# Seven block products in place of eight for part of gate and up, in both FFNs of a hybrid decoder layer

## Chip, cores and metric

One core of a Trainium2 chip. The metric is the time of one execution on the device in microseconds; smaller is better. Engines: TensorE (PE; PEld is its weight load), VectorE (DVE), ScalarE (ACT), GpSimd (POOL), and SyncE (SP), which issues DMAs.

## The reference, cut

256 tokens of width 2048 pass a SwiGLU half-step FFN, a stage of token mixers (convolution, latent attention, attention to memory, gates), and a second FFN. All is f32. The two FFNs are what the change touches:

```
def swiglu_ffn(h, w_gu, w_down):
    g, u = jnp.split(h @ w_gu, 2, axis=-1)
    return (jax.nn.silu(g) * u) @ w_down
x = x + 0.5 * swiglu_ffn(rmsnorm(x, g_ffn1[l]), w_ffn1_gu[l], w_ffn1_down[l])
...
x = x + 0.5 * swiglu_ffn(rmsnorm(x, g_ffn2[l]), w_ffn2_gu[l], w_ffn2_down[l])
```

`w_gu` is 2048 x 11264 (gate and up, 5632 columns each), `w_down` 5632 x 2048.

## The kernel before

Every f32 product is made of three passes in a reduced f32 type: both operands are split into a rounded part (h) and the rest (l), and h·h, l·h and h·l are summed in PSUM. Activations are the stationary operand (128 channels x 128 tokens), weights the moving one (128 x 512).

`linear` works off 512 output columns for the two token tiles: per chunk of two k tiles, `chunk` loads 512 KB of weights (`raw`, 4 buffers), ScalarE casts them to `wh` (line 139), VectorE subtracts for `wl` (line 141), and TensorE runs lines 163 to 165 per k tile and token tile. Two sums stand in two of four PSUM banks (`acc`), so the next `linear` starts in the other two.

`gate_up` takes 11 blocks of 512 columns. For each it calls `linear` for gate (16 k tiles), has ScalarE apply silu with the norm's factor (394), calls `linear` for up, and has VectorE multiply (398). `block_T` then turns the product h on TensorE (213) and splits it (192, 193), by deferred pieces: `defer` puts a closure into a queue that `tick` works off as chunks go by. In the first FFN's first block, `load_x` also loads x and has it turned; `setup_mixer` (constants and tables of the mixers) runs ahead of the silu of block 1. Then four `linear` calls with 44 k tiles take w_down, and add to x, which stays in SBUF.

The order of instructions on each engine is fixed ahead of time by a scheduler that takes what is ready, in program order; what is `pinned` keeps program order on its engine. Each engine works off its own queue in order. Tiles named `gen` share 32 buffers of 4 KB per partition; `misc` are four PSUM banks.

The mixers run between 545 and 1650 us; in them VectorE does the convolution with 360 operations (line 652) beside the splits of weights.

## Time and profile before

| what | value |
|---|---|
| median of 3 runs | 2455.03 us (2454.24 to 2455.8) |
| span of the profiled execution | 2454.7 us |
| TensorE, VectorE, ScalarE busy | 2443.1, 1415.3, 1129.7 us |
| matmuls, all forms | 11126 |
| mean DMA rate | 189 GB/s |

A busy share is an average over stages. Durations of matmuls overlap in the records, so their cost is read from start to start. A wait says which engine's instruction ended last before another could start.

### The profile page before, as it was taken

Reading aid. Unit: us, or ns where it says so; the run is one execution under the profiler, and the core shown is the slowest. Engines: PE = TensorE matmul, PEld = TensorE weight load, DVE = VectorE, ACT = ScalarE, POOL = GpSimd, SP = SyncE. Lnnn points to the kernel's source line nnn. Section 1 sums busy time; section 2 is a strip of 40 time slices with the busy share of each in tenths; the row PEclk is TensorE's granted clock in tenths of the full one; section 3 lists DMA queues with packets and bytes.
Section 4 is the critical chain, followed back from the end, with each engine's and each line's share of the span. In section 5 each row is a group of like instructions: output and inputs, shape, how many; then the busy total and the mean of one; then the engine's idle time right before and its main releaser. Section 6 shows DMA issues by size and latency. Waiting matters only on the chain.

```text
span 2454.7 us, 29412 instructions
## 1 busy us (share of the span) xinstructions
PE 2443.1 (100%) x11126; PEld 2025.3 (83%) x11126; DVE 1415.3 (58%) x1772; ACT 1129.7 (46%) x1476; POOL 77.5 (3%) x173
## 2 busy tenths in 40 slices
PE   8999999999999999999999999999999999999999
PEld 7888888888888889888888888888888888888887
DVE  5545545444445999975555576565545545444443
ACT  6444444444444455444556564344444444443332
POOL 2000000000000000000212100000000000000000
PEclk9999999999999999999999999999999999999999
DMA  7566666666667656565555567656666566666664
GB/s 244 184 192 191 188 190 189 189 189 199 200 200 231 188 182 181 187 195 150 173 151 168 163 180 239 198 182 186 189 189 189 188 190 192 186 191 192 200 203 138
DMA packets 240879, 463.63 MB, mean 189 GB/s; under 512 B 14752, under 2 KB 22544, under 8 KB 240736
## 3 DMA queue, kind: packets, MB, share of 16 engines
q1 hardware_dynamic: 236288, 449.89, 58.8%
q0 software_dynamic: 3264, 9.75, 1.4%
q10 hardware_dynamic: 1184, 2.11, 0.2%
q8 instruction: 87, 1.43, 0.2%
q14 instruction: 56, 0.46, 0.1%
HBM read 457.49 MB, written 4.19 MB: 188 GB/s over the span
## 4 chain that ended last, share of the span: by engine, by line
PE 97%; issue 2%; DMA 1%; POOL 0%; ACT 0%; SPq 0%; DVE 0%; POOLq 0%
PE acc L163 31%; PE acc L165 31%; PE acc L164 31%; PE misc L213 1%; PE misc L883 1%; DMA x<-in_x_dram 0%; PE misc L882 0%; PE misc L791 0%; PE misc L759 0%; POOL junk L274 0%; PE misc L863 0%; PE misc L912 0%; PE misc L905 0%; DMA junk<-in_g_mknorm_dram 0%; PE misc L745 0%
## 5 line engine op out<-in xcount | busy, mean ns | idle before, releaser
L141 DVE TENSOR_TENSOR wl<-raw,wh 128x1024 fp32r<-128x1024 f32 (+2 forms) x859 | 1043.9, 1217 | 935.8 <-ACT wh L139 930.4
L139 ACT CAST wh<-raw 128x1024 fp32r<-128x1024 f32 (+2 forms) x859 | 899.1, 1048 | 1183.8 <-PE acc L164 1124.4
L163 PE MATMUL acc<-wh,tH 128*128 128x512 f32 (+3 forms) x3200 | 1251.5, 391 | 1.4 <-ACT wh L139 1.4
L165 PE MATMUL acc<-wl,tH 128*128 128x512 f32 (+3 forms) x3200 | 1239.3, 387 | 0.0
L164 PE MATMUL acc<-wh,tL 128*128 128x512 f32 (+3 forms) x3200 | 1238.3, 387 | 0.0
L165 PEld LDWEIGHTS acc<-wl,tH 128*128 128x128 f32 x3200 | 601.8, 188 | 122.3
L163 PEld LDWEIGHTS acc<-wh,tH 128*128 128x128 f32 x3200 | 601.9, 188 | 121.7 <-issue 2.7
L164 PEld LDWEIGHTS acc<-wh,tL 128*128 128x128 f32 x3200 | 602.3, 188 | 117.6
L652 DVE SCALAR_TENSOR_TENSOR y<-aT,cw,y 128x256 f32<-128x256 f32 x360 | 150.2, 475 | 0.0
L394 ACT ACTIVATE sg<-acc,r 128x512 f32<-128x512 f32 x44 | 30.1, 690 | 25.2 <-PE acc L165 21.8
L195 ACT ACTIVATE tH<-misc,gains 128x256 fp32r<-128x256 f32 x56 | 26.0, 473 | 27.0 <-DVE tL L196 27.0
L163 PE MATMUL acc<-wh,oH 128*128 128x512 f32 x96 | 38.0, 395 | 0.0
L165 PE MATMUL acc<-wl,oH 128*128 128x512 f32 x96 | 37.4, 390 | 0.0
L164 PE MATMUL acc<-wh,oL 128*128 128x512 f32 x96 | 37.4, 389 | 0.0
L163 PE MATMUL acc<-wh,yH 128*128 128x512 f32 x96 | 37.3, 389 | 0.0
L164 PE MATMUL acc<-wh,yL 128*128 128x512 f32 x96 | 37.3, 389 | 0.0
L165 PE MATMUL acc<-wl,yH 128*128 128x512 f32 x96 | 37.3, 389 | 0.0
L193 DVE TENSOR_TENSOR tL<-misc,tH 128x512 fp32r<-128x512 f32 x44 | 30.1, 684 | 3.3 <-PE misc L213 3.3
L398 DVE SCALAR_TENSOR_TENSOR h<-acc,r,sg 128x512 f32<-128x512 f32 x44 | 31.4, 750 | 0.1
L196 DVE SCALAR_TENSOR_TENSOR tL<-misc,gains,tH 128x256 fp32r<-128x256 f32 x56 | 26.4, 479 | 8.7 <-ACT tH L195 8.7
L213 PEld LDWEIGHTS misc<-ident,h 128*128 128x128 f32 x176 | 21.8, 139 | 5.7
L213 PE MATMUL misc<-ident,h 128*128 128x128 f32 x176 | 26.3, 272 | 0.0
(215 smaller groups left out, 889.9 us busy)
## 6 DMA issues: line engine op xcount, KB each, us to landing
raw<-in_w_ffn_gu_dram SPq DMA_DIRECT2D x351, 512.0 KB, 3.5
raw<-in_w_ffn_down_dram SPq DMA_DIRECT2D x176, 512.0 KB, 4.1
raw<-in_w_in_dram SPq DMA_DIRECT2D x172, 512.0 KB, 3.7
raw<-in_w_mem_kv_dram SPq DMA_DIRECT2D x32, 512.0 KB, 4.2
raw<-in_w_out_dram SPq DMA_DIRECT2D x32, 512.0 KB, 3.7
raw<-in_w_conv_out_dram SPq DMA_DIRECT2D x24, 512.0 KB, 4.9
raw<-in_w_mla_out_dram SPq DMA_DIRECT2D x24, 512.0 KB, 4.1
raw<-in_w_mem_out_dram SPq DMA_DIRECT2D x16, 512.0 KB, 3.7
```

Source lines behind the costliest of these rows:

```text
L139: self.pinned(nc.scalar.copy(wh, raw))
L141: self.pinned(nc.vector.tensor_tensor(out=wl, in0=raw, in1=wh.bitcast(F32), op=ALU.subtract))
L163: nc.tensor.matmul(ps[tt], xh[:, t], wh[:, j, :], start=st, stop=False)
L164: nc.tensor.matmul(ps[tt], xl[:, t], wh[:, j, :], start=False, stop=False)
L165: nc.tensor.matmul(ps[tt], xh[:, t], wl[:, j, :], start=False, stop=sp)
L193: nc.vector.tensor_tensor(out=l, in0=src, in1=h.bitcast(F32), op=ALU.subtract)
L195: nc.scalar.activation(out=h, in_=src, func=AF.Identity, scale=scale)
L196: nc.vector.scalar_tensor_tensor(out=l, in0=src, scalar=scale, in1=h.bitcast(F32), op0=ALU.mult, op1=ALU.subtract)
L213: nc.tensor.transpose(ps[:, j, tt * P:(tt + 1) * P], src[:, tt, (j0 + j) * P:(j0 + j + 1) * P], self.ident)
L394: nc.scalar.activation(out=sg[:, tt], in_=pg[tt], func=AF.Silu, scale=rstd[:, tt:tt + 1])
L398: nc.vector.scalar_tensor_tensor(out=h[:, tt], in0=pu[tt], scalar=rstd[:, tt:tt + 1], in1=sg[:, tt], op0=ALU.mult, op1=ALU.mult)
L652: nc.vector.scalar_tensor_tensor(out=y, in0=aT[ch // 3][:, ch % 3, k:k + S], scalar=self.cw[:, ch, k:k + 1], in1=y, op0=ALU.mult, op1=ALU.add)
```

## The change

Gate and up of a block are now computed together, as one product over pairs of k tiles: 2 token tiles x 2 k tiles times 2 k tiles x (gate, up). `group` handles 8 pairs per block and keeps four sums F in all four `acc` banks. A plain pair takes 8 block products as before. In blocks 1 to 10 the pairs 0, 1 and 2 are computed with seven block products: `pair_chunk` forms four sums of weights on VectorE (three additions) and splits seven blocks of 512 columns; `pair_forms` forms the sums of the activations once per FFN, during block 0, after `prepare` has scaled x by the norm's factor; four of the seven products are summed in the four `misc` banks (`first`), three go to F (`second`); `remainders` makes the corrections E out of the four banks, and the end of the block adds E to F. The order of a block is Strassen, Strassen, plain, Strassen, four plain; `second` of the first pair comes behind `first` of the second.

Around it: weights are loaded 1 MB per pair into three `raw` slots; six slots each of `h` and `l`; one `t`. `ffn_stage` and `mix_stage` lay the same SBUF bytes out anew for the FFNs and for w_down with the mixers, where the slots have the old sizes. `gen` has 25 buffers, and seven more (`gen2`) lie in the mixers' layout. h is turned unsplit (`turn`, in the next block), and split by `h_fn` during the first `linear` of w_down; the first two weight chunks of w_down are made ahead of block 10's end. x is scaled in place, so it is loaded anew in the first FFN, and written to and read from DRAM (`xd2`) in the second. `setup_mixer`'s loads move to `load_mixer` after block 0; the rest runs after block 1 as before.

```diff
-NB_RAW = 4
-NB_H = 5
-NB_L = 5
-NB_GEN = 32
+NB_GEN = 25
+PAIRS = D // (2 * P)
+STRASSEN = (0, 1, 2)
+FFN_PLACES = [("raw", 8192)] * 3 + [("h", 4096)] * 6 + [("l", 4096)] * 6 + [("t", 6144), ("h4", 2048), ("h4", 2048),
+                                                                            ("l4", 2048), ("l4", 2048)]
...
+    def pair_chunk(self, W3, pr, b, seven, first=False):
...
+        def split(src, tags, n):
+            h = self.slot(tags[0], [n, CB], F32R)
+            self.pinned(nc.scalar.copy(h, src))
+            l = self.slot(tags[1], [n, CB], F32R)
+            self.pinned(nc.vector.tensor_tensor(out=l, in0=src, in1=h.bitcast(F32), op=ALU.subtract))
+            return [(h[:, i], l[:, i]) for i in range(n)]
...
+            return split(raw[:, 0:2], "hl", 2) + split(raw[:, 2:4], "hl", 2)
+        nc.sync.dma_start(out=raw[:, 0:2], in_=W3[ka, :, cs])
+        nc.sync.dma_start(out=raw[:, 2], in_=W3[kb, 1, cs])
+        nc.sync.dma_start(out=raw[:, 3], in_=W3[kb, 0, cs])
+        t = self.slot("t", [3, CB], F32)
+        add = lambda o, x, y: self.pinned(nc.vector.tensor_tensor(out=o, in0=x, in1=y, op=ALU.add))
+        add(t[:, 0:2], raw[:, 0:2], raw[:, 1:3])
+        add(raw[:, 1], t[:, 0], raw[:, 2])
+        add(t[:, 2], raw[:, 1], raw[:, 3])
+        b11, t2 = split(raw[:, 0:2], "hl", 2)
+        t1, t3 = split(t[:, 0:2], "hl", 2)
+        b22, b21 = split(raw[:, 2:4], "hl", 2)
+        (t4,) = split(t[:, 2:3], ("h4", "l4"), 1)
+        return b11, t2, t1, t3, b21, t4, b22
+    def pair_forms(self, xn, pr, g):
...
+        seven = pr in STRASSEN
+        ps = self.misc().rearrange("p (j t) -> p j t", j=4)
+        o = 2 * (pr % 2)
+        for j, (k, tt) in enumerate(((0, 0), (0, 1), (1, 1), (1, 0)) if seven else ((0, 0), (0, 1), (1, 0), (1, 1))):
...
+        x = self.gen([7, P], F32, "xf")
+        for k in range(2):
+            nc.scalar.activation(out=x[:, 2 * k:2 * k + 2], in_=ps[:, 2 * k:2 * k + 2], func=AF.Identity,
+                                 scale=g[:, 2 * pr + k:2 * pr + k + 1])
+        if not seven:
...
+            return [[(hl[:, 0, 2 * k + tt], hl[:, 1, 2 * k + tt]) for tt in range(2)] for k in range(2)]
+        v = nc.vector
+        v.tensor_tensor(out=x[:, 4:6], in0=x[:, 1:3], in1=x[:, 0:2], op=ALU.subtract)
+        v.tensor_tensor(out=x[:, 6], in0=x[:, 5], in1=x[:, 0], op=ALU.add)
+        v.tensor_tensor(out=x[:, 1], in0=x[:, 3], in1=x[:, 6], op=ALU.subtract)
+        h = self.gen([7, P], F32R, "xsH")
+        l = self.gen([7, P], F32R, "xsL")
...
+    def group(self, W3, b, forms, order, mid=None):
...
+        def first(w, f):
+            b11, t2, t1, t3, b21, t4, b22 = w
+            if not Q:
+                Q.extend(self.misc() for _ in range(4))
+                self.n7 = 0
+            st, sp = self.n7 == 0, self.n7 == n7 - 1
+            self.n7 += 1
+            for q, x, y in zip(Q, ("a11", "s6", "s5", "s7"), (b11, t2, t1, t3)):
+                self.mul(q, f[x], y, st, sp)
+        def second(w, f):
+            b11, t2, t1, t3, b21, t4, b22 = w
+            for i, x, y in ((0, "a12", b21), (1, "a22", t4), (2, "s3", b22)):
+                left[i] -= 1
+                put(i, f[x], y, left[i] == 0)
+        E = None
+        waiting = []
+        done = 0
+        for pos, (pr, seven) in enumerate(order):
+            f = forms(pr)
+            w = self.pair_chunk(W3, pr, b, seven, b == 0 and pos == 0)
+            if seven:
+                first(w, f)
+                done += 1
+                if pos == 0 and n7 > 1:
+                    waiting.append((w, f))
+                else:
+                    for a in waiting:
+                        second(*a)
+                    waiting = []
+                    second(w, f)
+            else:
+                plain(pr, w, f)
+            if n7 and done == n7 and E is None and not waiting:
+                E = self.remainders(Q)
+                Q = None
+            self.tick(4.0)
+            if mid is not None:
+                mid(pos)
+        return F, E
+    def remainders(self, Q):
...
+        E = self.slotE()
+        nc.scalar.copy(E[:, 0], p1)
+        v.tensor_tensor(out=E[:, 1], in0=q6, in1=E[:, 0], op=ALU.subtract)
+        v.tensor_tensor(out=E[:, 2], in0=E[:, 1], in1=p5, op=ALU.subtract)
+        v.scalar_tensor_tensor(out=E[:, 1], in0=E[:, 1], scalar=-1.0, in1=p7, op0=ALU.mult, op1=ALU.subtract)
+        v.tensor_tensor(out=E[:, 3], in0=E[:, 2], in1=p7, op=ALU.add)
+        def prepare(c):
+            rstd = self.get(rstd_)
+            xn = xs[c]
+            for tt in range(2):
+                nc.scalar.activation(out=xn[:, tt], in_=xn[:, tt], func=AF.Identity, scale=rstd[:, tt:tt + 1])
+            for pr in (2 * c, 2 * c + 1):
+                forms[pr] = self.pair_forms(xn, pr, gain)
+        def mid0(pos):
+            if mid is not None:
+                mid(pos)
+            if PAIRS - 5 <= pos < PAIRS - 1:
+                prepare(pos - (PAIRS - 5))
...
+        order0 = [(pr, False) for pr in range(PAIRS)]
+        rest = [pr for pr in range(PAIRS) if pr not in STRASSEN]
+        mixed = [(STRASSEN[0], True), (STRASSEN[1], True), (rest[0], False), (STRASSEN[2], True)]
+        mixed += [(pr, False) for pr in rest[1:]]
         for b in range(D_FF // CB):
-            pg = self.linear(W, b * CB, CB, xT, D // P, before if b == 0 else None)
-            rstd = self.get(rstd_)
-            if b == 1 and between is not None:
-                between()
+            if b == 0:
+                F, E = self.group(W3, b, plain_forms, order0, mid0)
+                rstd = self.get(rstd_)
+                scale = lambda tt: rstd[:, tt:tt + 1]
+            else:
+                F, E = self.group(W3, b, forms.get, mixed)
+            if between is not None and b < 2:
+                between[b]()
+            if b + 1 == D_FF // CB:
+                self.flush()
+                self.mix_stage()
+                hidden = self.h_fn(hT)
+                hidden(0)
+                ahead = [self.chunk(W_down, k0, 2, 0, CB) for k0 in (0, 2)]
             sg = self.gen([2, CB], F32, "sg")
-            for tt in range(2):
-                nc.scalar.activation(out=sg[:, tt], in_=pg[tt], func=AF.Silu, scale=rstd[:, tt:tt + 1])
-            pu = self.linear(W, D_FF + b * CB, CB, xT, D // P)
             h = self.gen([2, CB], F32, "h")
             for tt in range(2):
-                nc.vector.scalar_tensor_tensor(out=h[:, tt], in0=pu[tt], scalar=rstd[:, tt:tt + 1], in1=sg[:, tt],
-                                               op0=ALU.mult, op1=ALU.mult)
-            hT.append(self.block_T(h, lambda j: None, 1.5, 1.0))
-        return hT
+                if E is None:
+                    nc.scalar.activation(out=sg[:, tt], in_=F[tt], func=AF.Silu, scale=scale(tt))
+                else:
+                    nc.vector.tensor_tensor(out=sg[:, tt], in0=F[tt], in1=E[:, tt], op=ALU.add)
+                    nc.scalar.activation(out=sg[:, tt], in_=sg[:, tt], func=AF.Silu)
+            for tt in range(2):
+                if E is None:
+                    nc.vector.scalar_tensor_tensor(out=h[:, tt], in0=F[2 + tt], scalar=scale(tt), in1=sg[:, tt],
+                                                   op0=ALU.mult, op1=ALU.mult)
+                else:
+                    nc.vector.tensor_tensor(out=h[:, tt], in0=F[2 + tt], in1=E[:, 2 + tt], op=ALU.add)
+            if E is not None:
+                nc.vector.tensor_tensor(out=h, in0=h, in1=sg, op=ALU.mult)
+            self.defer(4.0 * 5 - 1 if b + 1 < D_FF // CB else 1.0, lambda h=h: turn(h))
+        return hidden, ahead
+        self.ffn_stage()
         for c in range(NCB):
-            ps = self.linear(d["w_ffn2_down"], c * CB, CB, self.xT_fn(hT), D_FF // P)
-            for tt in range(2):
-                nc.vector.scalar_tensor_tensor(out=xs[c][:, tt], in0=ps[tt], scalar=0.5, in1=xs[c][:, tt],
+            nc.gpsimd.dma_start(out=xd2[c], in_=xs[c])
+        hidden, ahead = self.gate_up(d["w_ffn2_gu"], blocks, xs, self.g_ffn2, rstd, d["w_ffn2_down"])
+        for c in range(NCB):
+            x = self.gen([2, CB], F32, "x2")
+            nc.gpsimd.dma_start(out=x, in_=xd2[c])
```

## Rows read from the trace of the kernel before

**Rows 1.** Page, parts 1 and 4: engines' busy time; shares of the chain.
```profile
PE 2443.1 (100%) x11126; PEld 2025.3 (83%) x11126; DVE 1415.3 (58%) x1772; ACT 1129.7 (46%) x1476; POOL 77.5 (3%) x173
...
PE acc L163 31%; PE acc L165 31%; PE acc L164 31%; PE misc L213 1%; PE misc L883 1%; DMA x<-in_x_dram 0%; PE misc L882 0%; PE misc L791 0%; PE misc L759 0%; POOL junk L274 0%; PE misc L863 0%; PE misc L912 0%; PE misc L905 0%; DMA junk<-in_g_mknorm_dram 0%; PE misc L745 0%
```

**Rows 2.** Page, part 5: line, xcount | busy us, mean ns | idle.
```profile
L163 PE MATMUL acc<-wh,tH 128*128 128x512 f32 (+3 forms) x3200 | 1251.5, 391 | 1.4 <-ACT wh L139 1.4
```

**Rows 3.** Waits, 45 to 485 us: total us, times, longest.
```profile
ACT wh L139 <- PE acc L164: 234.1, 144, 2.2
DVE wl L141 <- ACT wh L139: 207.0, 142, 1.6
```

**Rows 4.** Timeline of PE: start us, us, engine, line; 17 rows, first and last.
```profile
430.28 0.39 PE L165 MATMUL acc<-wl,tH 128*128 128x512 f32 x1
...
433.91 0.39 PE L163 MATMUL acc<-wh,tH 128*128 128x512 f32 x1
```

**Rows 5.** Timeline of PE around a group of transposes.
```profile
115.11 0.39 PE L165 MATMUL acc<-wl,tH 128*128 128x512 f32 x1
115.34 0.60 PE L213 MATMUL misc<-ident,h 128*128 128x128 f32 x4
...
116.01 0.39 PE L164 MATMUL acc<-wh,tL 128*128 128x512 f32 x1
```

**Rows 6.** VectorE's groups, shapes apart (columns as in rows 2).
```profile
L141 DVE TENSOR_TENSOR wl<-raw,wh 128x1024 fp32r<-128x1024 f32 x839 | 1024.8, 1224 | 923.3 <-ACT wh L139 917.8 <-PE misc L745 1.5
L460 DVE TENSOR_TENSOR x<-acc,x 128x512 f32<-128x512 f32 x8 | 5.5, 690 | 0.0
L658 DVE TENSOR_TENSOR lns<-y,y 128x1024 f32<-128x1024 f32 x1 | 1.2, 1215 | 0.0
```

**Rows 7.** Stretches: us, busy us (count) by engine, clock, DMA share.
```profile
820.00:1020.00 200.00, 200.00 (x994) 170.22 (x993) 199.97 (x377) 109.50 (x180) 3.77 (x6) 1.00 0.61 184
45.00:485.00 440.00, 439.73 (x1985) 363.44 (x1984) 227.16 (x239) 187.13 (x199) 1.01 (x2) 1.00 0.61 191
```

**Rows 8.** Timeline of VectorE in the convolution.
```profile
899.71 1.22 DVE L141 TENSOR_TENSOR wl<-raw,wh 128x1024 fp32r<-128x1024 f32 x1
900.85 1.67 DVE L652 SCALAR_TENSOR_TENSOR y<-aT,cw,y 128x256 f32<-128x256 f32 x4
```

**Rows 9.** ScalarE's groups, shapes apart (columns as in rows 2).
```profile
L139 ACT CAST wh<-raw 128x1024 fp32r<-128x1024 f32 x839 | 882.4, 1053 | 1162.1 <-PE acc L164 1105.5 <-issue 33.3 <-ACT e L893 4.7
L192 ACT CAST tH<-misc 128x512 fp32r<-128x512 f32 x44 | 25.6, 581 | 0.0
L195 ACT ACTIVATE tH<-misc,g 128x256 fp32r<-128x256 f32 x16 | 7.4, 472 | 8.4 <-PE misc L213 7.9 <-DVE tL L196 0.6
L139 ACT CAST wh<-raw 128x512 fp32r<-128x512 f32 x2 | 1.2, 617 | 0.5 <-DMA raw<-in_w_ffn_gu_dram 0.5
```

**Rows 10.** Timeline of ScalarE: one sum of squares.
```profile
28.02 0.63 ACT L185 ACTIVATE junk<-x 128x512 f32<-128x512 f32 x1
```

**Rows 11.** Timeline of the start, all engines, rows picked.
```profile
7.09 0.79 PE L163 MATMUL acc<-wh,tH 128*128 128x512 f32 x1 [1.44 <-ACT wh L139]
...
7.93 0.62 ACT L139 CAST wh<-raw 128x512 fp32r<-128x512 f32 x1 [0.52 <-DMA raw<-in_w_ffn_gu_dram]
...
14.82 0.66 PE L213 MATMUL misc<-ident,x 128*128 128x128 f32 x4 [2.24 <-DMA x<-in_x_dram]
...
20.01 0.48 PE L163 MATMUL acc<-wh,tH 128*128 128x512 f32 x1
```

**Rows 12.** Stretch of the start (columns as in rows 7).
```profile
16.00:19.40 3.40, 3.40 (x10) 2.61 (x9) 2.64 (x4) 2.45 (x3) 0.00 (x0) 0.51 1.05 386
```

**Rows 13.** Timeline of VectorE in the set-up of the mixers.
```profile
85.03 0.15 DVE L290 TENSOR_TENSOR g_nope<-gains 128x1 f32<-128x1 f32 x1
...
99.49 0.18 DVE L380 TENSOR_SCALAR ropeS<-ropeS 128x64 f32<-128x64 f32 x1
```

**Rows 14.** Page, part 6: issues, count, KB each, us to landing.
```profile
raw<-in_w_ffn_gu_dram SPq DMA_DIRECT2D x351, 512.0 KB, 3.5
```

More of the change, by code (lines that the diff above doesn't have):

```diff
@@ L86, in __init__, with ffn_stage @@
         self.pin = True
+    def ffn_stage(self):
+        old = self.rings
+        names = [t for t, _ in FFN_PLACES]
+        self.places(FFN_PLACES)
+        order = {t: [i for i, n in enumerate(names) if n == t] for t in dict.fromkeys(names)}
+        if old is not None:
+            for t, w, o in (("h", "wh", 3), ("l", "wl", 9)):
+                held = [p - o for p in self.was[w]]
+                order[t] = [o + i for i in [i for i in range(6) if i not in held] + held]
+        self.rings = order
+        self.place_of_g = None
@@ new lines, in places, with at @@
+    def places(self, sizes):
+        if self.slots is not None:
+            if self.place_of_g is not None:
+                for w in ("wh", "wl"):
+                    self.was[w] = [self.where[i] for i in self.rings[w]]
+            self.slots.close()
+        self.slots = ExitStack()
+        self.pools = [self.slots.enter_context(self.tc.tile_pool(name=self.nm(t), bufs=1)) for t, _ in sizes]
+    def at(self, i, shape, dt, name):
+        return self.pools[i].tile([P] + list(shape), dt, tag="p", name=self.nm(name))
@@ L148, in linear @@
         step = max(2, 1024 // N)
-        k0s = list(range(0, nk, step))
-        if before is not None:
-            k0s.insert(1, 1)
-        for k0, k1 in zip(k0s, k0s[1:] + [nk]):
-            if before is not None:
-                before(k0)
-            kk = k1 - k0
-            wh, wl = self.chunk(W, k0, kk, c0, N)
+        ahead = list(ahead)
+        for k0 in range(0, nk, step):
+            kk = min(step, nk - k0)
+            wh, wl = ahead.pop(0) if ahead else self.chunk(W, k0, kk, c0, N)
             for j in range(kk):
@@ new lines, in group, with put, plain @@
+    def group(self, W3, b, forms, order, mid=None):
+        nc = self.nc
+        F = [self.acc() for _ in range(4)]
+        begun = set()
+        n7 = sum(s for _, s in order)
+        left = {0: len(order), 1: len(order), 2: len(order), 3: len(order) - n7}
+        Q = []
+        def put(i, x, w, last):
+            self.mul(F[i], x, w, i not in begun, last)
+            begun.add(i)
+        def plain(pr, w, f):
+            for i in range(4):
+                left[i] -= 1
+            for k in range(2):
+                for g in range(2):
+                    for tt in range(2):
+                        i = 2 * g + tt
+                        put(i, f[k][tt], w[2 * k + g], k == 1 and left[i] == 0)
+        def first(w, f):
[10 more added lines that the diff above has]
+            for i, x, y in ((0, "a12", b21), (1, "a22", t4), (2, "s3", b22)):
+                left[i] -= 1
+                put(i, f[x], y, left[i] == 0)
[24 more added lines that the diff above has]
+        return F, E
@@ L438, in run, with load_x, turn_x, mid @@
-        hT = self.gate_up(d["w_ffn1_gu"], self.xT_fn(blocks), rstd, load_x, self.setup_mixer)
+        def load_x(c):
+            x = self.gen([2, CB], F32, "x")
+            n = CB // 2 if c == 0 else CB
+            for o in range(0, CB, n):
+                self.pinned(nc.sync.dma_start(out=x[:, :, o:o + n], in_=x_v[:, :, c * CB + o:c * CB + o + n]), True)
+            xs.append(x)
+        def turn_x(c):
+            blocks.append(self.block_T(xs[c], self.gains("g_ffn1", c), 0.0, 0.1))
+        def mid(pos):
+            self.pin = False
+            self.pin_dma = pos < 4
+            if pos < 3:
+                load_x(pos + 1)
+            if pos in (0, 2, 4):
+                turn_x(pos // 2 + 1)
+            if pos == 2:
+                self.stats(xs, D, 0.1, 0.1, True, rstd)
@@ L439, in run @@
+        (self.g_ffn1,) = self.load_gains([d["g_ffn1"]], "g1", nc.scalar)
+        load_x(0)
+        turn_x(0)
+        hidden, ahead = self.gate_up(d["w_ffn1_gu"], blocks, xs, self.g_ffn1, rstd, d["w_ffn1_down"], mid,
+                                     (self.load_mixer, self.setup_mixer))
         xd = [self.dp.tile([P, 2, CB], F32, tag=f"xd{c}", name=f"xd{c}") for c in range(NCB)]
+        xd2 = [self.dp.tile([P, 2, CB], F32, tag=f"xe{c}", name=f"xe{c}") for c in range(NCB)]
         blocks = []
+        xs = []
@@ L441, in run @@
         for c in range(NCB):
-            ps = self.linear(d["w_ffn1_down"], c * CB, CB, self.xT_fn(hT), D_FF // P)
+            x = self.gen([2, CB], F32, "x")
+            nc.gpsimd.dma_start(out=x, in_=x_v[:, :, c * CB:(c + 1) * CB])
+            xs.append(x)
+            ps = self.linear(d["w_ffn1_down"], c * CB, CB, hidden, D_FF // P, ahead if c == 0 else ())
             for tt in range(2):
```

189 lines of the change are left out of this document (147 added, 42 removed).

## The prediction

> **What bounds the kernel now.** I read the page first: TensorE is busy for the whole span, and the chain that ended last lies for 93% of the span on lines 163 to 165, the three passes of `linear` [rows 1]. VectorE (58%) and ScalarE (46%) have room on average [rows 1]. The groups of instructions then say how many matmuls these are: 3200 on each of the three lines, 9600 [rows 2]. The waits of ten FFN blocks confirm the direction: ScalarE waits for TensorE to free a `wh`, VectorE waits for ScalarE, and no wait of TensorE is among the long ones [rows 3]. So a matmul less is time less, as long as nothing else becomes late.
>
> The price of a matmul is not its mean of 391 ns, because records overlap. In the timeline 16 starts lie between 430.28 and 433.91 us [rows 4]: 3.63 / 16 = 0.227 us each. A group of four transposes, between two matmuls that start at 115.11 and 116.01 with one other in between, costs 0.90 - 2 x 0.227 = 0.45 us [rows 5]; its first follower starts late, and that is in it.
>
> **TensorE: removed and added.** One FFN block (512 gate and 512 up columns) now has 16 k tiles x 2 token tiles x 2 x 3 passes = 192 matmuls. After the change a plain pair has 24 and a Strassen pair 7 x 3 = 21, so blocks 1 to 10 have 5 x 24 + 3 x 21 = 183. Block 0 keeps 192. Removed: 9 x 10 blocks x 2 FFNs = 180 matmuls, 180 x 0.227 = **40.9 us**. Added: `pair_forms` transposes x a second time, 8 groups of four in each FFN, 16 x 0.45 = **7.2 us**. The transposes of h stay two groups per block. TensorE's time per mixed block is then 183 x 0.227 + 2 x 0.45 = 42.4 us, against 44.5 us. Net: -33.7 us, if TensorE stays fed.
>
> **VectorE: the new load.** Prices: a 1024-wide weight split 1.224 us, a 1024-wide f32 add 1.215, a 512-wide one that reads PSUM 0.690 [rows 6]; all 512-wide work is taken at 0.69. A plain pair is two splits, 2.45 us. A Strassen pair has the three weight additions, 1.215 + 2 x 0.69 = 2.60, and splits of 1024, 1024, 1024 and 512, 3 x 1.224 + 0.69 = 4.36: together 6.96 us. Per mixed block: 5 x 2.45 + 3 x 6.96 = 33.1; `remainders` 4 x 0.69 = 2.8; the end of the block 4 x 0.69 + 1.22 = 4.0. Sum 39.9 us in 40 instructions. In ten blocks of before VectorE is busy for 227 of 440 us, 52% [rows 7]; it goes to 39.9 / 42.4 = 94% of a block.
>
> Is that a bound? The stage where the convolution runs is the nearest row: from 820 to 1020 us VectorE is busy for 199.97 of 200 us, and TensorE for all 200 [rows 7]. A full VectorE therefore need not stop TensorE, if its order serves TensorE's weights first. And a full VectorE is faster than the sum of its durations: there a split starts at 899.71 and the next instruction at 900.85, 1.14 us later, though it lasts 1.22 [rows 8]. With 0.08 us of overlap at each of 40 instructions the block costs 36.7 us, 87% of TensorE's. I take no stall in the steady blocks. From below there is no gain to be had, since TensorE's waits there are already nil [rows 3]; the upper end is the rival below.
>
> The Trainium skill has a rule against this change. "VectorE: DVE Perf Modes", § The DRAIN you can't avoid, says that each operation is followed by a flush of roughly its duration less 266 ns before the next starts, and that chaining does not avoid it. By that rule, as an estimate, a mixed block would hold VectorE for about 39.9 + (39.9 - 40 x 0.266) = 69 us, and it would be the bound. This trace disagrees: the 1.14 us from start to start [rows 8] leave no room for a flush outside the recorded duration.
>
> **ScalarE.** Casts: plain pair 2 x 1.053, Strassen pair 3 x 1.053 + 0.617; `E`'s copy 0.58, two copies of h 2 x 0.58 [rows 9], two silu out of SBUF 2 x 0.63, as a square of the same size [rows 10]. Per mixed block 10.5 + 11.3 + 0.6 + 1.2 + 1.3 = 24.9 us of 42.4: hidden. The exception is block 0 of the first FFN. There `prepare` scales x (8 x 0.63), takes it turned out of PSUM (16 x 0.47), casts seven or four forms per pair (896 wide between 0.617 and 1.053, so 3 x 0.94, and 5 x 0.62), and this meets the sums of squares (8 x 0.63), the splits of x (16 x 0.47) and the block's own 16 casts (16.8). Sum 5.0 + 7.5 + 5.9 + 5.0 + 7.5 + 16.8 = 47.7 us against TensorE's 192 x 0.227 + 8 x 0.45 + 2.7 = 49.9 us. It has up to 6 `h` slots, three pairs, of lead. From 0 to 4 us; I take 1. In the second FFN x is turned earlier and the sum is 47.7 - 7.5 = 40 us: 0.
>
> **What is moved.** (a) The start. Now the first matmul starts at 7.09 us, on a 256 KB weight; the second weight's cast starts at 7.93 [rows 11]. After, the first cast takes gate and up of a k tile, 512 KB, and lasts 1.05: 7.93 + 1.05 = 9.0, 1.9 us later. In return the first pair has 24 matmuls, and x's second part is needed later. Before, 24 matmuls and two groups of transposes begin from 7.09 us on and ahead of the matmul at 20.01, so 12.92 - 24 x 0.227 - 2 x 0.45 = 6.6 us were lost: TensorE idles 2.24 us for x ahead of 14.82 [rows 11], and from 16.0 to 19.4 only ten records start, at a granted clock of 0.51, the lower of the two levels (1.2 GHz) [rows 12]. If the new start stays fed, it loses 1.9 us and half of some 4 to 7 us at the lower level, 3.9 to 5.4; with a further wait of 3 us for a transfer, 8.4; with the full clock from its first matmul on, 1.9. Against 6.6 that is -4.7 to +2; I take -1. The queue of SP carries x's parts between the weights as before, one per pair.
>
> (b) `setup_mixer` stays after block 1, but now VectorE is nearly full there and the four evacuations of block 1 are behind it in the program. Its chain of small operations runs from 85.03 to 99.67 us with four splits of weights in between (first and last of 34 rows [rows 13]): at most 14.6 - 4 x 1.14 = 10.0 us of VectorE, against a slack of 42.4 - 36.7 = 5.7 us. The next block's `second` waits for these evacuations and has 24 matmuls of `first`, 5.4 us, as cover. From 0 to 8 us, once; I take 3.
>
> (c) The splits of h go to the first `linear` of w_down: 11 x 1.05 us on ScalarE and 11 x 1.22 on VectorE beside 22 chunks that leave VectorE idle for 207.0 / 142 = 1.5 us each, by the blocks' own waits [rows 3]: hidden. Without that cover they would cost 13 us per FFN.
>
> (d) Buffers per stage. `raw` becomes three slots of 1 MB. A 512 KB transfer lands 3.5 us after its issue (median [rows 14]), and a slot is reloaded two pairs, some 10 us, ahead of its use: hidden. Three changes of layout, the same bytes for other tiles: each can make the first load wait for the last reader. From 0 to one such load and its cast, 3.5 + 1.05 = 4.6 us; the order in which slots are handed on puts free ones first, so I take 1 us in all, and up to 5 for the range. x read again and `xd2` written and read are 6 MB on POOL's queue, over some 1000 us: nothing, with the DMA engines at 0.61 in the FFN blocks [rows 7].
>
> **Sum** against the profiled execution: 2454.7 - 40.9 + 7.2 - 1 + 1 + 3 + 1 = 2425.0 us of span. The median of the runs lies 0.3 us above that span; I forecast **2425 us**. The bounds of these terms give 2455 - 33.7 - 4.7 = 2416 to 2455 - 33.7 + 2 + 4 + 8 + 5 = 2440.
>
> **The rivals.** *Short waits in each mixed block.* VectorE is in order, its order is fixed ahead of time, and it is 87 to 94% full. The evacuation of the four sums and the next pair's chain of 6.96 us meet within the 5.4 us of `first`. If one 1024-wide instruction (1.14 us) stands wrongly in front once per block: 20 x 1.14 = 23 us, 2448 us. For it: the tightness. Against it: the convolution, where as full a queue cost nothing [rows 7].
>
> *VectorE ahead by nothing, slower than before.* The six `h` and `l` slots hold two Strassen pairs, and `t` only one. If VectorE can't prepare a Strassen pair while TensorE is in plain pairs, each of the three costs 6.96 - 21 x 0.227 = 2.2 us of waiting, 6.5 us per block, 130 us in all: 2555 us. It decides from 30 / 20 = 1.5 us of waiting per block on: beyond that the kernel is slower than before. For it: slots are freed in turn, and the third Strassen pair needs what `second` holds. Against: two plain pairs leave 2 x (5.44 - 2.45) = 6 us for one Strassen pair's chain, and slots of two plain pairs are free by then.
>
> *A gap behind each VectorE instruction.* If one as long as the instruction followed each, a mixed block would hold VectorE for 2 x 39.9 = 80 us, 37 us more than TensorE needs: 750 us in all, 3170 us. The start of the next instruction 1.14 us after a 1.22 us one [rows 8] speaks plainly against it. The rule of the Trainium skill's "VectorE: DVE Perf Modes" named above is of this kind.
>
> *Fewer matmuls don't come out,* that is, the count in the trace stays at 9600: the bookkeeping of `left` and `begun` is plain in the diff; then 2455 plus the additions, 2466 us.
>
> **How the numbers follow.** Forecast 0.68; short waits 0.19; no lead 0.11; gaps 0.01; no fewer matmuls 0.01. About 0.2% (5 us) is what a measurement of this kernel can tell from no change. Faster than 2450: the forecast and most of the short waits, 0.83. Within: the rest of the short waits, 0.05. Slower: 0.12. Range: from the forecast's lower bound, 2416, to 2448, the short waits' middle; above lie 0.09 of those and the no-lead case.
>
> **What would show it.** 9420 matmuls of the three passes and 64 more transposes; a mixed block in 42.4 us; VectorE busy for about 39 us of it, and no long wait of TensorE for `wl` or the `h`, `l` tiles; TensorE's idle time in the block after `setup_mixer` below 8 us; the first matmul at about 9 us. Wrong would be a block of 44 us or more, with TensorE waiting for VectorE at each Strassen pair, or waits at the changes of layout of over 5 us.

## The result, and the profile of the changed kernel

The changed kernel takes **2424.45 us** (median; 2423.57 to 2425.59) beside 2455.41 us for the kernel before (2454.24 to 2455.8): a ratio of 0.9874, 95% interval [0.9860, 0.9888]. The gain of 31 us, 1.3%, is small but clear of the noise. The forecast was 2425 us. The profiled execution has a span of 2421.4 us, against 2454.7.

The profile page of the changed kernel, parts 1 and 4, in the columns of [rows 1]:

```profile
PE 2407.7 (99%) x11010; PEld 1998.1 (83%) x11010; DVE 1749.1 (72%) x2223; ACT 1277.9 (53%) x1701; POOL 84.0 (3%) x185
...
PE 95%; DVE 0%; issue 0%
```

TensorE has 11126 - 11010 = 116 records fewer: 180 matmuls removed, 64 transposes added. It still carries the chain. VectorE has gained 1749.1 - 1415.3 = 334 us of work, nearly ten times what TensorE lost, and none of that is on the chain: it shows 0% there.

The groups of the page for the FFNs' products and for VectorE's new work (columns as in [rows 2]):

```profile
L507 PE MATMUL acc<-h,xN 128*128 128x512 f32 x800 | 313.1, 391 | 0.0
...
L494 DVE TENSOR_TENSOR t<-raw 128x1024 f32<-128x1024 f32 x120 | 114.5, 954 | 17.4 <-DMA raw<-in_w_ffn_gu_dram 16.1
L509 PE MATMUL misc<-l,xsH 128*128 128x512 f32 x240 | 93.4, 390 | 2.0 <-DVE l L477 2.0
L507 PE MATMUL misc<-h,xsH 128*128 128x512 f32 x240 | 93.7, 391 | 0.8 <-ACT h L475 0.7
```

The 240 on a line with `misc` are `first`: 4 products x 3 pairs x 20 blocks. They wait 2.0 + 0.8 us in the whole run. L494 are the weight additions, the new work of VectorE that the chain doesn't see.

Two stretches of whole mixed blocks, seven of the first FFN (7 x 42.37 = 296.6 us) and ten of the second, in the columns of [rows 7]:

```profile
151.76:448.38 296.62, 296.62 (x1339) 246.30 (x1337) 260.15 (x282) 167.74 (x189) 0.00 (x0) 1.00 0.58 199
1753.39:2177.00 423.61, 423.61 (x1911) 351.79 (x1910) 368.52 (x395) 242.18 (x273) 0.60 (x1) 1.00 0.58 200
```

From one block's first matmul to the next's it is 42.37 us in both FFNs. TensorE is busy in every microsecond of both stretches, VectorE 260.15 / 7 = 37.2 us per block, 88% (52% in [rows 7]), ScalarE 24.0 us. The waits of TensorE over the whole run (total us, times, longest) are few:

```profile
PE misc L351 <- POOL invf L402: 3.2, 1, 3.2
PE acc L507 <- ACT h L475: 2.6, 1, 2.6
PE misc L509 <- DVE l L477: 2.0, 2, 1.0
PE misc L507 <- ACT h L475: 0.7, 1, 0.7
PE acc L507 <- ACT sg L688: 0.5, 1, 0.5
```

The first two lie ahead of the first matmul. The other three all lie between 63 and 71 us, where block 0 of the first FFN hands over to block 1. That is the only place where the change costs TensorE a wait, and the experiments from "Where block 1 of the first FFN begins" on are about it.

### The profile page after: what moved, and what is told of

Read it like the earlier page. It is cut to its first block, busy times and chain, and to the rows that moved or that the text cites. A ratio compares the mean times of both kernels' runs of the same rounds, so it can differ in the third digit from the quotient of the medians.

```text
span 2421.4 us, 30174 instructions
## 1 busy us (share of the span) xinstructions
PE 2407.7 (99%) x11010; PEld 1998.1 (83%) x11010; DVE 1749.1 (72%) x2223; ACT 1277.9 (53%) x1701; POOL 84.0 (3%) x185
## 4 chain that ended last, share of the span: by engine, by line
PE 95%; DVE 0%; issue 0%
PE acc L229 19%; PE acc L231 19%; PE acc L230 19%; PE acc L509 9%; PE acc L508 9%; PE acc L507 9%; PE misc L507 2%; PE misc L509 2%; PE misc L508 2%; PE misc L661 1%; PE misc L279 1%; PE misc L1220 1%; PE misc L1219 0%; PE misc L1128 0%; PE misc L1096 0%; PE misc L1200 0%
## 5 line engine op out<-in xcount | busy, mean ns | idle before, releaser
L210 DVE TENSOR_TENSOR wl<-raw,wh 128x1024 fp32r<-128x1024 f32 (+1 forms) x506 | 612.2, 1214 | 447.4 <-ACT wh L208 444.3
L208 ACT CAST wh<-raw 128x1024 fp32r<-128x1024 f32 (+1 forms) x506 | 528.3, 1046 | 650.2 <-PE acc L230 592.4
L229 PE MATMUL acc<-wh,tH 128*128 128x512 f32 (+3 forms) x1792 | 697.0, 389 | 0.5 <-DVE gate L961 0.5
L231 PE MATMUL acc<-wl,tH 128*128 128x512 f32 (+3 forms) x1792 | 690.0, 385 | 0.0
L230 PE MATMUL acc<-wh,tL 128*128 128x512 f32 (+3 forms) x1792 | 689.4, 385 | 0.0
L475 ACT CAST h<-raw 128x1024 fp32r<-128x1024 f32 x352 | 367.7, 1052 | 282.8 <-PE acc L508 172.8
L477 DVE TENSOR_TENSOR l<-raw,h 128x1024 fp32r<-128x1024 f32 x352 | 425.7, 1219 | 64.1 <-ACT h L475 61.0
L507 PE MATMUL acc<-h,xN 128*128 128x512 f32 x800 | 313.1, 391 | 0.0
L509 PE MATMUL acc<-l,xN 128*128 128x512 f32 x800 | 311.6, 389 | 0.0
L508 PE MATMUL acc<-h,xN 128*128 128x512 f32 x800 | 311.5, 389 | 0.0
L507 PEld LDWEIGHTS acc<-h,xN 128*128 128x128 f32 x800 | 150.3, 188 | 30.5
L508 PEld LDWEIGHTS acc<-h,xN 128*128 128x128 f32 x800 | 150.3, 188 | 30.4
L494 DVE TENSOR_TENSOR t<-raw 128x1024 f32<-128x1024 f32 x120 | 114.5, 954 | 17.4 <-DMA raw<-in_w_ffn_gu_dram 16.1
```

Source lines behind the costliest of these rows:

```text
L208: self.pinned(nc.scalar.copy(wh, raw))
L210: self.pinned(nc.vector.tensor_tensor(out=wl, in0=raw, in1=wh.bitcast(F32), op=ALU.subtract))
L229: nc.tensor.matmul(ps[tt], xh[:, t], wh[:, j, :], start=st, stop=False)
L230: nc.tensor.matmul(ps[tt], xl[:, t], wh[:, j, :], start=False, stop=False)
L231: nc.tensor.matmul(ps[tt], xh[:, t], wl[:, j, :], start=False, stop=sp)
L475: self.pinned(nc.scalar.copy(h, src))
```

## Experiments

My theory: what a pair saves is the issue time of its three matmuls, 0.68 us of a block, as long as VectorE's work, from start to start, fits in TensorE's block; buffers and order matter little. The rivals: the new layout or the lead carries part of the gain or of the risk (order of the pairs), and VectorE's limit is the sum of its durations. The first four runs change the number of pairs, with an order to suit.

**No pair with seven products.**

```diff
-STRASSEN = (0, 1, 2)
+STRASSEN = ()
...
+                scale = lambda tt: 1.0
```

> No pair is computed with seven products; everything else of the changed kernel stays (gate and up together, buffers per stage, x transposed a second time). Theory (TensorE's matmuls set the time): 180 matmuls x 0.227 = 40.9 us come back, and the 4.6 us that TensorE waits at the start of block 1 go, since VectorE has less to do there: a span of 2458 to 2462 us. Rival (the new order and layout are what gave the time): 2421 to 2435 us.

Measured: a time of 2467.4 us (span 2465.6, above the 2462 expected), against 2454.28 before. So layout, joint gate and up, and start give nothing by themselves; with the second turning of x they cost 13 us. 7.2 of it are the transposes, and most of the rest is a wait, which the expectation did not have (longest wait of TensorE in this kernel):

```profile
PE acc L507 <- ACT sg L689: 5.1, 2, 4.5
```

Block 1, plain here, needs the `acc` banks at once, and these wait for block 0's silu. The whole gain of the change is in the seven products.

**Two pairs, and four.**

```diff
-STRASSEN = (0, 1, 2)
+STRASSEN = (0, 1)
...
+        mixed = [(left7.pop(0), True) if s == 'S' else (left8.pop(0), False) for s in 'SSNNNNNN']
```

```diff
-STRASSEN = (0, 1, 2)
+STRASSEN = (0, 1, 2, 3)
...
+        mixed = [(left7.pop(0), True) if s == 'S' else (left8.pop(0), False) for s in 'SSNSNSNN']
...
-            self.defer(4.0 * 5 - 1 if b + 1 < D_FF // CB else 1.0, lambda h=h: turn(h))
+            self.defer(4.0 * 7 - 1 if b + 1 < D_FF // CB else 1.0, lambda h=h: turn(h))
```

The second of these also turns h two pairs later.

> Two of eight pairs with seven products instead of three. Theory: one pair less is 3 matmuls x 20 blocks x 0.227 = 13.6 us: a span of 2433 to 2435 us, a mixed block of 43.1 us. Rival (the time is from order and layout): 2421 to 2425 us.

> Four of eight pairs with seven products (order S S N S N S N N). VectorE has 44.4 us of durations per mixed block, 40.8 us if each of 45 instructions overlaps the next by 0.08; TensorE has 180 x 0.227 + 0.9 = 41.8 us. Theory (VectorE bounds by start-to-start time): TensorE still sets the pace, 13.6 us less and 0 to 6 us of new waits: a span of 2408 to 2414 us. Rival (VectorE bounds by the sum of its durations): 44.4 us per block, 20 x 2.0 = 40 us more, 2462 us. Rival (too little lead, short waits at each pair): 2421 to 2440 us.

Measured: spans 2436.0 us (1 us above what was expected) and 2421.9 us (theory: 2408 to 2414); the latter's median is 2424.0 us, ratio 0.9877 [0.9861, 0.9894]. Steady blocks take 43.05, 42.37 and 41.72 us with two, three and four pairs: 0.68 and 0.65 us per pair, three matmuls at 0.227. The same 300 us of the second FFN, with two, three and four pairs, each in its own kernel:

```profile
1800.00:2100.00 300.00, 300.00 (x1353) 249.16 (x1352) 233.01 (x245) 155.00 (x174) 0.00 (x0) 1.00 0.59 196
```

```profile
1800.00:2100.00 300.00, 300.00 (x1354) 249.12 (x1353) 263.22 (x284) 168.95 (x191) 0.00 (x0) 1.00 0.58 200
```

```profile
1800.00:2100.00 300.00, 300.00 (x1353) 249.06 (x1352) 295.49 (x325) 178.13 (x211) 0.00 (x0) 1.00 0.59 198
```

VectorE per block: 233.01 x 43.05 / 300 = 33.4 us, then 37.2, then 41.1. A pair costs it 3.8 to 3.9 us; it saves TensorE 0.68. At four pairs it holds 41.1 of 41.72 us and TensorE doesn't stop in this stretch. But four pairs bring nothing over three in total. 6.9 us more than with three pairs are lost where block 1 of the first FFN begins (11.5 us between 60 and 110 us, against 4.6; how this is counted stands below). Blocks 3, 4 and 7 of the first FFN take 42.4 to 42.8 us instead of 41.72, block 1 of the second FFN takes 43.17, and the two starts of w_down wait 0.7 us each. So the span lies in the range of the third rival, too little lead, but its waits come where the load begins and in single blocks, not at each pair.

**Five pairs.**

```diff
-STRASSEN = (0, 1, 2)
+STRASSEN = (0, 1, 2, 3, 4)
...
+        mixed = [(left7.pop(0), True) if s == 'S' else (left8.pop(0), False) for s in 'SSNSSNSN']
...
-            self.defer(4.0 * 5 - 1 if b + 1 < D_FF // CB else 1.0, lambda h=h: turn(h))
+            self.defer(4.0 * 8 - 1 if b + 1 < D_FF // CB else 1.0, lambda h=h: turn(h))
```

> Five of eight pairs with seven products (order S S N S S N S N). VectorE: 49.0 us of durations, 45.0 us start to start in 50 instructions; TensorE 41.1 us. Theory: VectorE is now the bound, 45.0 us per mixed block against 42.4 with three pairs, 20 x 2.6 = 52 us more: a span of 2465 to 2485 us, VectorE busy all through the mixed blocks. Rival (bound by durations): 49.0 us per block, 2553 us. Rival (VectorE still has slack): 2394 us.

Measured: span 2488.7 us (a time of 2490.51 us): slower than before. Steady blocks take 44.85 us where TensorE needs 41.04. The block came out as expected; the span is 4 us above the expected range, and the waits at the two starts of w_down (the second line of waits below) are 13.0 us that the expectation did not have. A stretch of the first FFN (columns as in [rows 7]), then the longest waits of TensorE, and ScalarE's longest between 150 and 450 us:

```profile
150.00:450.00 300.00, 285.95 (x1236) 223.36 (x1235) 298.79 (x336) 178.77 (x207) 0.00 (x0) 1.00 0.56 186
```

```profile
PE misc L507 <- ACT h L475: 17.9, 33, 4.1
PE acc L229 <- DVE sg L690: 13.0, 2, 6.7
PE acc L507 <- DVE sg L690: 12.0, 13, 1.0
```

```profile
ACT h L475 <- DVE t L494: 86.1, 37, 3.9
```

VectorE is full (298.79 of 300) and TensorE is not: the bound has moved. Its place is where the start-to-start price says: 41.1 + 3.9 = 45.0 us of VectorE per block. The sum of durations, 39.9 + 2 x (6.96 - 2.45) = 48.9 us, is refuted by 44.85. So is, far more, the flush as the prediction read it in the Trainium skill's "VectorE: DVE Perf Modes", § The DRAIN you can't avoid: as an estimate by that rule these 50 instructions would take about 48.9 + (48.9 - 50 x 0.266) = 84 us. The same section also says that a next operation that is not held starts earlier; the prediction left that out, and it is the case that 44.85 us agrees with. The ScalarE named in the first wait is itself waiting for `t`, which VectorE's weight additions form (the last line).

**Three pairs in a row.**

```diff
-        mixed = [(STRASSEN[0], True), (STRASSEN[1], True), (rest[0], False), (STRASSEN[2], True)]
-        mixed += [(pr, False) for pr in rest[1:]]
+        left7, left8 = list(STRASSEN), list(rest)
+        mixed = [(left7.pop(0), True) if s == 'S' else (left8.pop(0), False) for s in 'SSSNNNNN']
```

> The same three pairs with seven products, but in a row at the head of each block (S S S N N N N N in place of S S N S N N N N): the same work on every engine, less lead for VectorE. It has 3 x 6.4 = 19.2 us start to start for them, TensorE 3 x 4.8 = 14.3. Theory (the spread of the pairs gives VectorE its lead; slots allow two Strassen pairs ahead): 1 to 2 us of waiting per mixed block, a span of 2441 to 2461 us. Rival (only VectorE's total per block matters, 88%): 2421 to 2424 us.

Measured: span 2425.0 us, steady blocks of 42.47 us against 42.37. My theory of the lead falls here: the slots carry VectorE over three Strassen pairs in a row for 0.1 us per block. The rival, that the order hardly matters in a steady block, stands. The rest of the 3.6 us lies early in the first FFN, in block 1 (49.34 us against 48.21) and block 3 (43.15).

**Where block 1 of the first FFN begins.** From the changed kernel, TensorE's rows at the handover (block 1's first matmul starts at 61.04):

```profile
63.54 0.39 PE L509 MATMUL misc<-l,xsH 128*128 128x512 f32 x1
64.67 0.50 PE L507 MATMUL misc<-h,xsH 128*128 128x512 f32 x1 [0.74 <-ACT h L475]
...
65.47 0.40 PE L508 MATMUL misc<-h,xsL 128*128 128x512 f32 x1
66.86 0.73 PE L509 MATMUL misc<-l,xsH 128*128 128x512 f32 x2 [1.00 <-DVE l L477]
...
69.74 0.73 PE L509 MATMUL misc<-l,xsH 128*128 128x512 f32 x2 [1.02 <-DVE l L477]
70.97 0.50 PE L507 MATMUL acc<-h,xsH 128*128 128x512 f32 x1 [0.50 <-ACT sg L688]
```

The first pair's `first` runs through (12 matmuls, 2.7 us); the second pair's weights then come one by one. Counting 0.2268 us for each matmul that starts and 0.1125 (a quarter of 0.45) for each transpose, TensorE falls behind by 2.87 us up to 60 us and by 7.42 us up to 110: 4.6 us are lost here, all of them ahead of 72 us. I first blamed one engine's load. Two kernels moved some to GpSimd:

```diff
-                nc.scalar.activation(out=xn[:, tt], in_=xn[:, tt], func=AF.Identity, scale=rstd[:, tt:tt + 1])
+                nc.gpsimd.tensor_scalar(out=xn[:, tt], in0=xn[:, tt], scalar1=rstd[:, tt:tt + 1], scalar2=None, op0=ALU.mult)
```

> The eight scalings of x in prepare go from ScalarE to POOL (5.3 us of ScalarE's time in block 0 of each FFN). It asks what makes TensorE wait 4.6 us in all at the start of block 1 of the first FFN. Theory 1 (ScalarE's load in block 0): the waits fall to 1.5 us or less, a span of 2417 to 2419 us. Theory 2 (VectorE's load): the waits stay, 2421 us, or grow by what POOL is slower.

```diff
-        v = nc.vector
+        v = nc.gpsimd
```

> The nine additions that form sums of activations in pair_forms go from VectorE to POOL (2.9 us of VectorE's time in block 0 of each FFN). Theory 2 (VectorE's load in block 0 makes TensorE wait at the start of block 1): the waits of 4.6 us fall by 2 to 3 us, a span of 2418 to 2419 us. Theory 1 (ScalarE's load): unchanged, 2421 us.

Measured: spans 2429.9 and 2430.1 us, both slower than the changed kernel, and for a reason that leaves the question open: GpSimd takes longer for the same work. The scalings' group (1962 ns each; 720 on ScalarE) and the wait that they cause, in the first kernel, and the largest group of additions in the second (1110 ns each; 420 on VectorE):

```profile
L642 POOL TENSOR_SCALAR x<-x,r 128x512 f32<-128x512 f32 x16 | 31.1, 1962 | 8.1 <-PE misc L279 7.9
```

```profile
PE misc L518 <- POOL x L642: 4.1, 2, 3.6
```

```profile
L529 POOL TENSOR_TENSOR xf<-xf 128x256 f32<-128x256 f32 x6 | 6.7, 1110 | 36.1 <-ACT xf L521 36.1
```

Inconclusive, then: the cover was lost and new waits took its place. The next two leave the work out instead.

```diff
+            if pin and c > 0:
+                self.nc.gpsimd.memset(ss[:, :, c:c + 1], 1.0)
+                return
...
-        v.tensor_tensor(out=x[:, 4:6], in0=x[:, 1:3], in1=x[:, 0:2], op=ALU.subtract)
-        v.tensor_tensor(out=x[:, 6], in0=x[:, 5], in1=x[:, 0], op=ALU.add)
-        v.tensor_tensor(out=x[:, 1], in0=x[:, 3], in1=x[:, 6], op=ALU.subtract)
+        nc.gpsimd.memset(x[:, 4:7], 1.0)
```

The first three lines are the kernel without squares, the others the one without additions.

> Left out: the sums of squares of three of x's four parts in the first FFN (6 of 8 squares, a constant stands in their place), 6 x 0.62 and their readouts, 4.9 us of ScalarE in block 0. It asks again what makes block 1 of the first FFN last 48.2 us instead of the 43.7 that its matmuls and the set-up's transposes need. Theory 1 (ScalarE is late there): the 4.6 us of waits go, block 1 lasts 43.7 to 44.5 us, a span of about 2417 us. Theory 2 (VectorE alone is late): block 1 stays at 47.5 us or more, 2421 us. Both full together: something between.

> Left out: the nine additions in pair_forms of each FFN (a constant stands for three of the seven forms), 2.9 us of VectorE in block 0. Theory 2 (VectorE is late in block 0 of the first FFN): the waits at block 1's start fall by 2 to 3 us, block 1 lasts 45 to 46.5 us, a span of 2418 to 2419 us. Theory 1 (ScalarE alone is late): block 1 stays at 47.5 us or more, 2421 us.

Measured: spans of 2422.8 us for both (times of 2424.59 and 2424.55 us), where the kernel before took 2457.99 us (one run). The count of lost time above compares them better, since it leaves the start out. Neither theory's gain came in the span. Stretches of 44 to 72 us (columns as in [rows 7]) of the changed kernel, without squares, without additions:

```profile
44.00:72.00 28.00, 24.73 (x114) 18.87 (x113) 27.67 (x37) 26.94 (x43) 6.63 (x14) 1.00 0.51 167
```

```profile
44.00:72.00 28.00, 24.64 (x116) 19.47 (x115) 27.93 (x37) 26.30 (x42) 6.76 (x14) 1.00 0.56 179
```

```profile
44.00:72.00 28.00, 24.50 (x110) 19.02 (x109) 25.35 (x31) 26.55 (x43) 6.79 (x14) 0.94 0.50 160
```

In the changed kernel VectorE (27.67 of 28 us) and ScalarE (26.94) are both full. The squares lie too early, so that leaving them out hardly relieves ScalarE here; without the additions VectorE has 2.65 us to spare, and ScalarE, still full, has not. The loss by the same count is 5.7 and 4.7 us.

These counts hold something that the changed kernel's 4.6 us don't. In both kernels TensorE waits once for longer (2.94 us without squares, 2.62 without additions, against at most 1.02 in the changed kernel), and behind it the granted clock falls to its lower level and matmuls start 0.43 us apart. Without squares, then without additions:

```profile
71.80:75.40 3.60, 3.60 (x10) 2.83 (x9) 3.60 (x6) 1.64 (x2) 0.00 (x0) 0.53 0.85 302
```

```profile
69.50:71.80 2.30, 2.25 (x6) 1.84 (x7) 2.27 (x4) 2.30 (x3) 0.00 (x0) 0.55 0.00 0
```

About 1.7 us of each loss lie in these stretches. Without them, as an estimate, 4.0 and 3.0 us are lost against 4.6: the additions' 1.6 us are near the 2 to 3 of theory 2, the squares' 0.6 far from theory 1. With one execution of each kernel, that is a hint and no proof. Relieving both at once:

```diff
+            if mid is not None and c > 1:
+                forms[2 * c] = forms[2 * c + 1] = forms[3]
+                return
```

> Left out: in the first FFN alone the second half of x isn't scaled, turned and split for the blocks behind block 0 (pairs 4 to 7 use pair 3's tiles); four groups of transposes, 1.8 us of TensorE, go with it, and some 8 us of ScalarE and 3 us of VectorE between 46 and 62 us. Matmuls of the three passes stay as many. Theory 1, the load of both engines late in block 0 makes the second Strassen pair of block 1 late: the 4.6 us lost between 60 and 80 us shrink to at most 1 us, span 2421.4 - 1.8 - 3.6 = 2416 us (2415 to 2417). Theory 2, the loss belongs to block 1's start whatever ran ahead of it (slots handed on, silu of block 0 behind the casts): only the transposes go, 2419.6 us (2419 to 2421).

Measured: span 2418.7 us, between the two theories. ScalarE falls to 20.85 us, VectorE only to 26.97:

```profile
44.00:72.00 28.00, 26.48 (x116) 20.67 (x115) 26.97 (x37) 20.85 (x29) 0.00 (x0) 1.00 0.59 192
```

The loss is 2.5 us instead of 4.6, at a granted clock of 1.00 in both. So about half of it was the load of the second half of `prepare`. Whether the other half belongs to the handover itself isn't shown: the first half of `prepare` is still there, and VectorE is still at 26.97 of 28 us.

**Four pairs, with block 1 of the first FFN plain.** Here the forms of the second half of x move from block 0 into block 1:

```diff
-STRASSEN = (0, 1, 2)
+STRASSEN = (0, 1, 2, 3)
...
+            elif pos in (4, 6):
+                prepare(pos // 2 - 2)
...
+        def mid1(pos):
+            if pos in (0, 2):
+                prepare(pos // 2 + 2)
...
+                if mid is not None and b == 1:
+                    F, E = self.group(W3, b, plain_forms, order0, mid1)
```

> Four pairs with seven products (order S S N S N S N N), and in the first FFN block 1 stays plain, with the forms of x prepared in blocks 0 and 1 instead of in block 0 alone. Theory (four pairs are still paced by TensorE once block 1 of the first FFN isn't overloaded): against the changed kernel 19 mixed blocks x 0.68 = 13 us less, block 1 plain 9 matmuls = 2.0 us more, the 4.6 us of waits at its start gone or nearly: a span of 2406 to 2412 us. Rival (with VectorE at 98% every mixed block waits a little): 2416 to 2424 us.

Measured: **2414.61 us** (2414.03 to 2415.66), ratio 0.9837 [0.9821, 0.9854] to the kernel before, span 2413.9: the fastest of all, 9.8 us less than the changed kernel, though above the 2412 that my theory allowed. Steady blocks take 41.72 us in both FFNs (block 1 of the second 43.17, where TensorE waits 1.0 us for the forms of x); a stretch of the first:

```profile
150.00:440.00 290.00, 290.00 (x1309) 240.62 (x1308) 285.24 (x314) 171.68 (x203) 0.00 (x0) 1.00 0.60 203
```

VectorE is 98% full and TensorE is never idle there. The handover still loses 4.3 us, now because a plain block needs the `acc` banks at once (the wait in this kernel, and ScalarE's timeline that ends it; TensorE goes on at 63.64):

```profile
PE acc L507 <- ACT sg L698: 2.3, 1, 2.3
```

```profile
61.61 1.28 ACT L698 ACT_TABLE_LOAD   x1
62.90 1.27 ACT L698 ACTIVATE sg<-acc,r 128x512 f32<-128x512 f32 x2
```

1.28 of these 2.3 us are a table load that ScalarE makes ahead of its first silu; making it earlier was not tried. Most of the rest of the 4.3 us is the clock again: it reads 0.54 from 64.4 to 68.1 us, and 1.7 us are lost there.

**Four pairs, Strassen in block 1 too.** As the last, but block 1 takes its four Strassen pairs first, and the plain pairs' forms are made behind them:

```diff
-            if pos in (0, 2):
-                prepare(pos // 2 + 2)
+            if pos in (3, 5):
+                prepare((pos + 1) // 2)
...
-                    F, E = self.group(W3, b, plain_forms, order0, mid1)
+                    F, E = self.group(W3, b, forms.get, [(pr, pr in STRASSEN) for pr in range(PAIRS)], mid1)
```

> Four Strassen pairs as before with block 1 among the Strassen blocks again (four in a row, then four plain pairs); block 0 prepares only the forms of pairs 0 to 3, those of the four plain pairs are made in block 1, behind the corrections. Against the kernel with four pairs and a plain block 1 (span 2413.9): 12 matmuls fewer, -2.7 us. Theory 1 (the load late in block 0): the 4.3 us that are lost there at the start of block 1 fall to about 1, and the forms of pair 4, which now stand directly ahead of their use, cost 0 to 3: 2407 to 2411 us of span. Theory 2 (the start of block 1 loses its time whatever ran ahead): 4.3 us stay, and the forms' wait comes on top: 2411 to 2414.

Measured: 2418.59 us (2417.7 to 2419.98), ratio 0.9852 [0.9836, 0.9869], span 2418.2: both expectations missed. It loses 9.0 us from 60 to 110: 4.4 us in one wait, 2.8 in matmuls that start 0.43 us apart behind it, and 1.6 us around the forms of pair 4. Its longest wait of TensorE, the stretch behind it (columns as in [rows 7]), and the timeline of VectorE and ScalarE that leads to the wait's end:

```profile
PE misc L507 <- ACT h L475: 4.4, 1, 4.4
```

```profile
69.62:75.39 5.77, 5.76 (x14) 4.23 (x15) 3.95 (x5) 4.53 (x6) 0.00 (x0) 0.51 0.31 120
```

```profile
66.49 0.69 DVE L477 TENSOR_TENSOR l<-t,h 128x512 fp32r<-128x512 f32 x1
67.21 1.23 DVE L494 TENSOR_TENSOR t<-raw 128x1024 f32<-128x1024 f32 x1
...
68.53 1.04 ACT L475 CAST h<-t 128x1024 fp32r<-128x1024 f32 x1 [4.50 <-DVE t L494]
```

ScalarE is idle for 4.50 us here, so it isn't what is short. VectorE begins the second pair's weight additions when the first pair's last split has left the one `t` (66.49 + 0.69 = 67.18, then 67.21). But it has been busy without a gap up to there, with the forms' additions and splits in between, and the additions stand behind that split in its pinned order anyway: what is short is VectorE's time, and a second `t` alone need not have helped (not tried). This is the "no lead" rival in small: at the handover VectorE is no pair ahead, and `first` of one pair is all the cover.

## Why the prediction was right, step by step

**TensorE's sum** held: 116 records fewer as counted, 42.37 us for a mixed block against 42.4, and the series of two, three and four pairs gives 0.65 to 0.68 us per pair, the price of [rows 4].

**VectorE** was the term with the risk. Predicted 36.7 us per block by start-to-start time, measured 37.2; the sum of durations was 39.9. The overlap of 0.08 us read at one place of the convolution [rows 8] held for a whole block, and five pairs showed that it is this time that decides. That a full VectorE needn't stop TensorE [rows 7] held at 98% in steady blocks; with four pairs some of the first blocks still lost time. In the changed kernel the short waits of the first rival didn't come in any steady block; "no lead" didn't either, nor when three pairs stood in a row.

**The start** was taken at -1 (-4.7 to +2) and came to -3.2: the first matmul starts at 8.19 us, 1.1 later than in [rows 11], and TensorE then falls 2.3 us behind its own pace up to 20 us, against 6.6 before. The wait for x of 2.24 us and the stretch at 0.51 [rows 12] are gone. The 4 to 7 us at the lower level that the prediction added here stand in no row. From 8.19 to 12.62, 4.4 us, matmuls start mostly 0.43 us apart, then at 0.227:

```profile
12.20 0.63 PE L507 MATMUL acc<-h,tH 128*128 128x512 f32 x1
12.62 0.53 PE L508 MATMUL acc<-h,tL 128*128 128x512 f32 x1
12.99 0.40 PE L509 MATMUL acc<-l,tH 128*128 128x512 f32 x1
13.22 0.39 PE L507 MATMUL acc<-h,tH 128*128 128x512 f32 x1
```

**Block 0 of the first FFN** was the mis-sized term: +1 (0 to 4) predicted, +4.6 measured, just outside its bounds. The failed step is the balance of ScalarE over the whole block, 47.7 of 49.9 us. The work isn't spread over the block: it stands in its last part, where ScalarE is at 26.94 of 28 us. And VectorE, at 27.67 of 28 us there, was left out of the sum for this block. Leaving the second half of `prepare` out took about 2 us of the 4.6 away. What the other 2.5 us are stays open: the rest of `prepare`, the one `t`, the six slots and the little cover that `first` gives were not tried apart.

**`setup_mixer`** was taken at +3 (0 to 8), as VectorE's slack seemed too small for it. It cost 0.14 us: block 2 takes 42.51 us. VectorE's rows there show why: the small operations go in one by one between the evacuations, instead of ahead of them.

```profile
110.82 0.22 DVE L411 TENSOR_TENSOR rope<-posf,invf 128x64 f32<-128x64 f32 x1
110.95 0.68 DVE L690 TENSOR_TENSOR sg<-acc,E 128x512 f32<-128x512 f32 x1
111.56 0.18 DVE L417 TENSOR_SCALAR rope<-rope 128x64 f32<-128x64 f32 x1
111.65 0.68 DVE L690 TENSOR_TENSOR sg<-acc,E 128x512 f32<-128x512 f32 x1
```

**Layouts and hidden transfers:** no wait of TensorE lies at a change of layout: 0, where I had taken 1 (0 to 5). The splits of h beside w_down and the reading of `xd2` cost TensorE nothing either.

So four small terms were off by -2.2, +3.6, -2.9 and -1: -2.5 us together, which takes 2425.0 to 2422.5 us of span. The measured 2421.4 leaves 1.1 us. A tail behind the last matmul that is 0.5 us shorter, and blocks that went from 44.47 to 42.37 us, 0.06 us more than nine matmuls are worth, cover that. In spans the sum missed by 3.6 us. The time came out right by 0.6 us partly because the errors cancel and partly by luck: the prediction set the time 0.3 us above the span, but each execution of the changed kernel took 2.1 to 2.2 us more than its own span (2423.57 beside 2421.4). The two large terms, -40.9 and +7.2, and the absence of waits in the steady blocks are what was really foreseen.

## What to carry to other kernels

To trade work of a full engine for work of one with room, price the latter from start to start in a stretch where it is already full, and compare block by block: here it may go to 98% at no cost in a steady block, and one step further (five pairs) the whole gain is lost and more. Then look for the place where the new load begins; there no lead has been built up, two engines' loads add up in a part of one block, and an average over the block hides it. A variant that is better in every steady block (four pairs) won nothing until that place was eased, here by a plain block ahead of the first Strassen one. And when variants are compared by lost time, look at the granted clock first: what follows a wait can cost as much as the wait.
